# TensorE's written order: ready tasks of the loaded tile shape first, value products held back somewhat

## The chip, the cores and the metric

One Trainium2 chip; the kernel runs on one of its cores. The metric is device microseconds of one execution (us). The kernel before was timed in three runs; the median counts.

## What is computed

One encoder layer over two requests with the same weights, 4096 and 2048 tokens of 1024 features. Cut to what matters here:

```python
proj = rms_norm(x, norm_g) @ w_in                       # 1024 -> 3072 columns, split into the heads' parts
ya = neighbourhood_attention(qa, ka, va, rpb) * silu(na_g)   # 6 heads, 8 rows x 16 columns of a 64-wide grid
yb = windowed_gqa(qb, kb, vb, sink) * silu(wg)               # 6 query heads, 2 key heads, |t-s| <= 128
yc = memory_attention(qc, km, vm) * silu(mg)                 # 4 heads into 256 memory tokens
return x + concatenate([ya, yb, yc]) @ w_out
```

Every attention is a score product, a softmax over the keys and a value product. Queries and keys are normalised per head before the scores.

## The kernel before, in words

The tokens are worked off in 24 groups of 256 (16 of the first request, 8 of the second), each of two blocks of 128. Every matrix product is done in float16 pieces, a high and a low part of each operand, as three products that add up in one PSUM bank.

The first stage holds the weights for neighbourhood and memory attention. Per block it turns the input over on TensorE, four 128x128 transposes at a time (label xT, L527), projects it (labels pga and pgb of 512 columns and pgv of 384, L302 to L305: 24 matmuls each), normalises queries and keys on VectorE and GpSimd, and turns those over on TensorE (qT, L729). Per group there are then six units of neighbourhood attention: three head pairs by two pairs of column blocks. A unit is a score product on TensorE (qk, L903), bias and maximum on VectorE (L920), the exponential on ScalarE (L930), the scaling into a high and a low part on ScalarE and VectorE (L956, L965), one transposing DMA from SP's queue that writes the tile pt (L971), and the value product on TensorE (pv, L986), which waits for that DMA. Memory attention has the same chain with the labels mqk (L1042), mpT (L1092, tile ptm) and mpv (L1104), two of each per group. The raw attention results go out to HBM and are read again in the second stage, which has windowed attention (wqk, L1321; wpv, L1373), the gates (gate, L1270 to L1272), a projection of 320 columns (tok, L302 to L305 on wa and x) and the output projection (out, L1448 to L1450).

Nothing of this order is written out by hand. The class Plan keeps a list of tasks, each with an engine, a planned duration, a priority, the tasks that it needs and the buffers that it takes and gives back. Its run() goes through planned time: whenever an engine is free, it takes from that engine's ready tasks the one with the lowest priority number whose buffers are free, records its instructions, and marks the engine busy for the planned duration. A task with a slack above zero becomes ready that many planned microseconds after its last need is met. The order in which tasks are recorded is the order in which each engine works at run time; there every instruction waits only for its data. SP's DMA queue is such an engine too, and it issues in the recorded order.

TensorE's matmuls come in four shapes of array use, given in the profile as rows*columns: 128*128 for projections, gates, outputs and transposes, 64*64 for qk, 64*128 for mqk and wqk, and 128*64 for pv, mpv and wpv (96 rows in part of pv). The plan before knows nothing of them. Buffers that matter: four banks for scores (sc), two for value products (po), two for projections (pj, a third from the second stage on), four pt tiles.

Of the kernel before, what the change touches and what calls it, by code (L numbers as in the profile page):

```python
# [41 lines left out]


class Task:
    __slots__ = ("eng", "dur", "fn", "prio", "lat", "acq", "rel", "nd", "succ", "idx", "label", "slack", "xf", "start", "run", "need")

# [3 lines left out]
         "rcp": -0.1, "sc1": 2.9, "sc3": -1.24, "tab": 0.82, "ttr": -0.2, "vld": 0.2, "vst": -1.0, "w2l": -0.07,  # L52
         "wh": 3.15, "wl": 2.66, "wload": 0.43, "wmax": -1.05, "wpv": -0.5, "wqk": -1.0, "wsq": 0.93, "x": -0.53,
         "x2": -1.0,  "xrs": -0.04, "xss": 0.55, "xst": 1.74}


class Plan:
# [11 lines left out]
    def add(self, eng, dur, fn, deps=(), prio=0.0, lat=None, acq=(), rel=(), label="", slack=0.0, xf=0.0):  # L69


        t = Task()
        t.eng = t.run = eng
        t.dur, t.fn, t.prio = dur, fn, prio + SHIFT.get(label, 0.0)
        t.lat = {"pe": 0.2, "dve": 0.13, "act": 0.13, "pool": 0.16, "free": 0.01}.get(eng, 0.1) if lat is None else lat
        t.acq, t.rel, t.succ = tuple(acq), tuple(rel), []
        names = [a[0] if isinstance(a, tuple) else a for a in acq]
        t.need = tuple((a, names.count(a)) for a in dict.fromkeys(names))
        t.idx, t.label, t.xf, t.slack, t.start = len(self.tasks), label, xf, slack, None
        if label.endswith("T"):  # L80
            t.xf *= 1.5
        if eng == "sp" and xf > 0:
            t.dur = (0.63 if label.endswith("T") else 0.45) * round(dur / 0.1)
        ds = [d for d in deps if d is not None]
        t.nd = len(ds)
        for d in ds:
            d.succ.append(t)
        self.tasks.append(t)
        return t
# [21 lines left out]
    def run(self):  # L111
        avail = self.avail = dict(self.caps)
        ready = {t.eng: [] for t in self.tasks}
        busy = {}
# [17 lines left out]
        now = 0.0  # L132
        done = 0
        dma_free = 0.0
        while done < len(self.tasks):
            progress = True
            while progress:
                progress = False
                for e, q in ready.items():
                    if busy.get(e, 0.0) > now or not q:  # L140
                        continue
                    skipped = []
                    pick = None
                    while q and pick is None and len(skipped) < 25:
                        item = heapq.heappop(q)
                        if all(avail[a] >= n for a, n in item[2].need):
                            pick = item[2]
                        else:
                            skipped.append(item)
                    for s in skipped:  # L150
                        heapq.heappush(q, s)
                    if pick is None:
                        continue
                    progress = True
                    self.acquire(pick)
                    pick.start = now
                    self.emit(pick)
                    busy[e] = now + pick.dur
                    at(busy[e], FREE, pick)
                    if pick.xf > 0:  # L160

                        at(now + (0.71 if pick.label.endswith("T") else 0.53 if e == "sp" else pick.dur) + 0.65, MOVE, pick)
                        if pick.label.endswith("T"):
                            busy[e] = 1e9
                    else:
                        at(now + pick.dur + pick.lat, DONE, pick)
            if not ev:
                left = [t.label for q in ready.values() for _, _, t in q][:20]
                raise RuntimeError(f"no progress at {now}: {left} {avail}")
            now = ev[0][0]  # L170
            while ev and ev[0][0] <= now:
                _, _, kind, t = heapq.heappop(ev)
                if kind == READY:
                    heapq.heappush(ready[t.eng], (t.prio, t.idx, t))
                elif kind == MOVE:
                    dma_free = max(now, dma_free) + t.xf
                    at(dma_free + 0.95, DONE, t)
                    if t.label.endswith("T"):

                        busy[t.eng] = max(now, dma_free - 0.9)  # L180
                        at(busy[t.eng], FREE, t)
                elif kind == DONE:
                    done += 1
                    self.release(t)
                if kind == DONE or (kind == FREE and t.xf == 0):

                    for s in t.succ:
                        if (s.eng == t.eng and t.xf == 0) == (kind == FREE):
                            s.nd -= 1
                            if s.nd == 0:  # L190
                                push(now, s)
# [3 lines left out]
def build(tc, A, out, seqs):  # L195
# [64 lines left out]
    pl = Plan()  # L260
# [585 lines left out]
    for gs_ in range(NSB):  # L846
# [25 lines left out]
        for hp in range(3):  # L872
            t_pvs = []
            for ab in range(2):
# [8 lines left out]
                def f_s(us=us, cbs=cbs, kw=kw, nrows=nk // kw, kgs=kgs, hp=hp, gs_=gs_):  # L883
# [11 lines left out]
                    for r0, nr in runs:  # L895
# [7 lines left out]
                                    T.matmul(bank("sc", us[j])[64 * half:64 * half + 64, ko:ko + nr * kw], qa, ka,  # L903
                                             start=(pi == 0), stop=(pi == 2))
                        ko += nr * kw
                t_s = pl.add("pe", (3 * nk / 2.4 + 200) / 1000, f_s, base, prio=pru, acq=[("sc", u) for u in us], label="qk")
                last_qk.append(t_s)
                for h in (2 * hp, 2 * hp + 1):
                    u = (gs_, h, ab)
# [65 lines left out]
                def f_pv(gs_=gs_, hp=hp, ab=ab, kgs=kgs, edge=edge):  # L975
# [4 lines left out]
                    for half, cb in enumerate(PAIRS[ab]):  # L980
                        for ci, k in enumerate(kgs):
                            K = 96 if ab == 0 and not edge and ci == 2 else 4 * CB_KW[cb]
                            for vv in ((0, 1) if ci < nc_ - 1 else (1, 0)):
                                for j in range(2):
# [2 lines left out]
                                             st["va", k][0:K, cb, vv * 384 + h * 64:vv * 384 + h * 64 + 64],  # L987
                                             pt[0:K, j, ci, 0:2 - vv, 64 * half:64 * half + 64].rearrange("p a (r c) -> p a r c", c=16),
                                             start=(ci == 0 and vv == 0), stop=(ci == nc_ - 1 and vv == 0))
                t_pv = pl.add("pe", 0.82 * len(kgs) / 3, f_pv, [t_pT] + (vdep if ab == 0 else []) + t_pvs[-1:],  # L990
                              prio=pru, acq=[("po", gs_, hp)] if ab == 0 else [], rel=["pt"], label="pv", slack=0)
                t_pvs.append(t_pv)
                last_pv.append(t_pv)

# [27 lines left out]
    for gs_ in range(NSB):  # L1022
# [10 lines left out]
        for blk in range(2):  # L1033
            us = [(gs_, hp, blk) for hp in range(2)]

            def f_s(us=us, s=s, gs_=gs_, blk=blk):

                for j in range(2):
                    for pi, (qv, kv) in enumerate(((0, 0), (0, 1), (1, 0))):
                        for hp in range(2):  # L1040
# [1 line left out]
                            T.matmul(bank("sc", "m", us[hp])[:, 256 * j:256 * j + 256],  # L1042
                                     st["qn", 2 * gs_ + blk][prt, j, qv, :],
                                     mkv_t[s][0][prt, 2 * kv + j, :], start=(pi == 0), stop=(pi == 2))
            t_s = pl.add("pe", 0.85, f_s, [qm_done[2 * gs_ + blk], t_T1] + t_mk, prio=prm + blk / 2.0, acq=[("sc", "m", u) for u in us],
                         label="mqk")
            mqk.append(t_s)
            t_sb.append(t_s)
        for hp in range(2):
# [47 lines left out]
            def f_pv(gs_=gs_, hp=hp, s=s):  # L1097
                po = bank("po", "m", gs_, hp)[:, 0:256]
                pt = st["ptm", gs_, hp]
                for ci in range(2):  # L1100
                    for pi, (pp, vv) in enumerate(((0, 0), (0, 1), (1, 0))):
                        for j in range(2):
                            h = hp + 2 * j
                            T.matmul(po[64 * j:64 * j + 64, :], mkv_t[s][1][:, ci, vv, h * 64:h * 64 + 64],  # L1104
                                     pt[:, j * 4 + pp * 2 + ci, :], start=(ci == 0 and pi == 0), stop=(ci == 1 and pi == 2))
            t_pv = pl.add("pe", 0.82, f_pv, t_pts, prio=prm + hp / 2 + 0.25, acq=[("po", "m", gs_, hp)], rel=["ptm"], label="mpv")
            mem_use.append(t_pv)
            ym_use.append(t_pv)

# [178 lines left out]
    for nb in range(NB):  # L1288
# [10 lines left out]
        for jh in range(6):  # L1299
# [4 lines left out]
            if kv == 0:  # L1304
                us = [(nb, j), (nb, 3 + j)]

                def f_s(us=us, kbs=kbs, nb=nb, j=j):
# [9 lines left out]
                    for r0, nr in runs:  # L1317
                        for pi, (qv, kk) in enumerate(((0, 0), (0, 1), (1, 0))):
                            for v in range(2):
# [1 line left out]
                                T.matmul(bank("sc", "w", us[v])[:, o:o + nr * P], st["qT", nb][prt, 3 * qv + j, :],  # L1321
                                         st["ring2"][prt, kk, r0 * P:(r0 + nr) * P], start=(pi == 0), stop=(pi == 2))
                        o += nr * P
                t_s = pl.add("pe", (3 * nk / 2.4 + 220) / 1000, f_s, [k_done[k] for k in kbs] + [q2_done[nb], t_T3], prio=pru,
                             acq=[("sc", "w", u_) for u_ in us], label="wqk")
                win_qk[nb].append(t_s)

# [39 lines left out]
        def f_pv(nb=nb, kbs=kbs, nch=nch):  # L1367
            po = bank("po", "w", nb)
            pt = st["ptw", nb]
            for ci, k in enumerate(kbs):  # L1370
                for pi, (pp, vv) in enumerate(((0, 0), (0, 1), (1, 0))):
                    for kv in range(2):
# [1 line left out]
                                 st["vw", k][:, vv, 64 * kv:64 * kv + 64],  # L1374
                                 pt[:, pp * nch + ci, 3 * kv:3 * kv + 3, :],
                                 start=(ci == 0 and pi == 0), stop=(ci == nch - 1 and pi == 2))
        t_pv = pl.add("pe", 0.188 * 3 * nch, f_pv, t_pts + [v2_done[k] for k in kbs], prio=prw + 0.5, acq=[("po", "w", nb)], rel=["pt2"], label="wpv")
        win_pv[nb] = t_pv
        pl.add("free", 0.0, lambda: None, win_qk[nb], rel=["qT2"], label="f")

# [177 lines left out]
```

## Time and profile before

| | before |
|---|---|
| median of 3 runs | 2723.16 us (2718.52 to 2727.7) |
| the profiled execution's own time | 2732.95 us |
| its span, first to last instruction | 2731.1 us |
| mean granted TensorE clock | 0.978 |
| TensorE busy | 2590.1 us (95%) |
| VectorE, ScalarE, GpSimd busy | 1879.7, 1272.5, 543.4 us |

A row of a timeline gives start and length of an instruction or of a run of like ones, and in brackets how long the engine stood idle before it and what ended that. The lengths of matmuls overlap: how fast TensorE goes is read from the distance of the starts. PE is TensorE, DVE VectorE, ACT ScalarE, POOL GpSimd, SP the queue that issues most DMAs. The first stage runs to about 1250 us of the span, the second from there; from about 1180 us the last units of the first overlap with the first projections of the second.

### The profile page before, as it was taken

Reading aid. Unit: us, or ns where it says so; the run is one execution under the profiler, and the core shown is the slowest. Engines: PE = TensorE matmul, PEld = TensorE weight load, DVE = VectorE, ACT = ScalarE, POOL = GpSimd, SP = SyncE. Lnnn points to the kernel's source line nnn. Section 1 sums busy time; section 2 is a strip of 40 time slices with the busy share of each in tenths; the row PEclk is TensorE's granted clock in tenths of the full one; section 3 lists DMA queues with packets and bytes.
Section 4 is the critical chain, followed back from the end, with each engine's and each line's share of the span. In section 5 each row is a group of like instructions: output and inputs, shape, how many; then the busy total and the mean of one; then the engine's idle time right before and its main releaser. Section 6 shows DMA issues by size and latency. Waiting matters only on the chain.

```text
span 2731.1 us, 58589 instructions
## 1 busy us (share of the span) xinstructions
PE 2590.1 (95%) x22150; PEld 1600.3 (59%) x22150; DVE 1879.7 (69%) x5370; ACT 1272.5 (47%) x3685; POOL 543.4 (20%) x738
## 2 busy tenths in 40 slices
PE   5989888999998899978999999999999999999999
PEld 3545454555554555556666666666666666666665
DVE  6477777888777778885865665666666656566664
ACT  7456555666666667673433333333333333333332
POOL 2553233333322543321000000000000000000000
PEclk9999999999999999988999999999999999999999
DMA  5488997989998998899645444454454435455443
GB/s 182 141 160 175 190 194 186 188 191 201 206 198 181 212 212 168 169 211 261 143 101 105 100 107 106 110 122 112 111 113 104 104 90 106 106 112 122 109 95 76
DMA packets 707467, 401.38 MB, mean 147 GB/s; under 512 B 617648, under 2 KB 654160, under 8 KB 706544
## 3 DMA queue, kind: packets, MB, share of 16 engines
q1 hardware_dynamic: 691312, 347.10, 60.7%
q0 software_dynamic: 15872, 50.55, 5.4%
q8 instruction: 173, 2.83, 0.4%
q14 instruction: 110, 0.90, 0.1%
HBM read 160.54 MB, written 87.03 MB: 91 GB/s over the span
## 4 chain that ended last, share of the span: by engine, by line
PE 56%; DMA 1%; DVE 1%; issue 0%; ACT 0%; POOL 0%; SPq 0%; DVEq 0%; ACTq 0%; POOLq 0%
PE bank L1270 7%; PE bank L1448 6%; PE bank L1271 6%; PE bank L1272 6%; PE bank L1449 6%; PE bank L1450 6%; PE bank L302 4%; PE bank L303 4%; PE bank L305 4%; PE bank L1321 3%; PE bank L1373 3%; DMA pt<-phl 1%; DVE phl L965 0%; PE bank L986 0%; DVE pf L920 0%
## 5 line engine op out<-in xcount | busy, mean ns | idle before, releaser
L1270 PE MATMUL bank<-x,wb 128*128 128x256 f16 x1152 | 315.2, 274 | 0.0
L1271 PE MATMUL bank<-x,wb 128*128 128x256 f16 x1152 | 314.0, 273 | 0.0
L1272 PE MATMUL bank<-x,wa 128*128 128x256 f16 x1152 | 314.0, 273 | 0.0
L1338 ACT ACTIVATE pf<-pf,sm 128x384 f32<-128x384 f32 (+1 forms) x288 | 172.6, 599 | 300.6 <-DVE sm L1332 299.5
L302 PE MATMUL bank<-wa,xT 128*128 128x512 f16 x768 | 299.3, 390 | 4.4 <-DVE vhl L689 3.8
L303 PE MATMUL bank<-wa,xT 128*128 128x512 f16 x768 | 297.9, 388 | 0.7 <-DVE wa L364 0.6
L1448 PE MATMUL bank<-wo,yT 128*128 128x512 f16 x768 | 291.3, 379 | 0.0
L1449 PE MATMUL bank<-wo,yT 128*128 128x512 f16 x768 | 291.1, 379 | 0.0
L1450 PE MATMUL bank<-wo,yT 128*128 128x512 f16 x768 | 291.1, 379 | 0.0
L309 POOL TENSOR_TENSOR r<-r,wA 128x8 f32<-128x8 f32 x48 | 10.3, 215 | 1276.3 <-DVE r L1223 1276.3
L1277 ACT ACTIVATE tg<-bank,hg 128x256 f32<-128x256 f32 x192 | 89.6, 467 | 364.0 <-PE bank L1272 364.0
L311 POOL TENSOR_TENSOR r<-r,mhalf 128x16 f32<-128x16 f32 (+2 forms) x100 | 223.8, 2238 | 7.8
L930 ACT ACTIVATE pf<-pf,sm 128x288 f32<-128x288 f32 (+3 forms) x288 | 156.1, 543 | 128.0 <-DVE sm L920 125.9
L302 PE MATMUL bank<-wa,x 128*128 128x320 f16 x768 | 213.3, 301 | 1.0 <-DMA x<-xTd 1.0
L303 PE MATMUL bank<-wa,x 128*128 128x320 f16 x768 | 213.0, 301 | 0.0
L1463 DVE SCALAR_TENSOR_TENSOR xr<-bank,oc,xr 128x512 f32<-128x512 f32 x96 | 71.9, 749 | 197.8 <-PE bank L1450 197.8
L1332 DVE CUSTOM_DVE_ANT_0 pf<-bank,wtab,nsink 128x384 f32<-128x384 f32 (+1 forms) x288 | 163.9, 599 | 58.6 <-PE bank L1321 58.5
L302 PEld LDWEIGHTS <-xT 128*128 128x128 f16 x1152 | 115.2, 100 | 124.8 <-issue 25.1
L303 PEld LDWEIGHTS <-xT 128*128 128x128 f16 x1152 | 115.1, 100 | 114.5 <-issue 16.3
L305 PE MATMUL bank<-wa,xT 128*128 128x512 f16 x768 | 181.4, 379 | 0.0
L305 PEld LDWEIGHTS <-xT 128*128 128x128 f16 x1152 | 112.8, 98 | 115.7 <-issue 0.3
L1355 DVE SCALAR_TENSOR_TENSOR phl<-pf,sm,phl 128x384 f16<-128x384 f32 (+1 forms) x288 | 174.3, 605 | 8.5
(261 smaller groups left out, 5746.1 us busy)
## 6 DMA issues: line engine op xcount, KB each, us to landing
xTd<-xT POOLq DMA_DIRECT2D x48, 512.0 KB, 4.7
x<-xTd SPq DMA_DIRECT2D x48, 512.0 KB
out<-xr SPq DMA_DIRECT2D x48, 512.0 KB
xx<-in_x_prompt SPq DMA_DIRECT2D x32, 512.0 KB
xr<-in_x_prompt SPq DMA_DIRECT2D x32, 512.0 KB
od<-oev POOLq DMA_DIRECT2D x120, 128.0 KB, 3.8
ot<-od SPq DMA_DIRECT2D x120, 128.0 KB
vd<-vhl POOLq DMA_DIRECT2D x48, 192.0 KB, 4.4
```

The source lines that it names most:

```text
L302: T.matmul(ps, xt[:, kk], wh[:, kk, cols], start=(kk == 0), stop=False)
L303: T.matmul(ps, xt[:, kk], wl[:, kk, cols], start=False, stop=False)
L305: T.matmul(ps, xt[:, NK + kk], wh[:, kk, cols], start=False, stop=(kk == NK - 1))
L311: G.tensor_tensor(out=r, in0=r, in1=mhalf[:, 0:n], op=ALU.pow)
L1270: T.matmul(pv, wh, x[:, :, kk, :], start=(kk == 0), stop=False)
L1271: T.matmul(pv, wh, x[:, :, NK + kk, :], start=False, stop=False)
L1272: T.matmul(pv, wl, x[:, :, kk, :], start=False, stop=(kk == NK - 1))
L1338: S.activation(out=pf[:, 0:nk], in_=pf[:, 0:nk], func=AF.Exp, scale=-1.0, bias=sm[:, 0:1], accum_out=sm[:, 1:2])
L1355: V.scalar_tensor_tensor(out=phl[:, nk:2 * nk], in0=st["pfw", u][:, 0:nk], scalar=st["smw", u][:, 3:4], in1=phl[:, 0:nk], op0=ALU.mult, op ...
L1448: T.matmul(ps, yT[:, 0, ts_], st["wo0"][:, c, cs], start=(ci == 0), stop=False)
L1449: T.matmul(ps, yT[:, 0, ts_], st["wo1"][:, c, cs], start=False, stop=False)
L1450: T.matmul(ps, yT[:, 1, ts_], st["wo0"][:, c, cs], start=False, stop=(ci == 7))
```

## The change

Three things, all inside the plan; no instruction is added, removed or resized.

First, a task on TensorE has a shape. When the pick of lowest priority has another shape than the task before it, run() looks on through the ready tasks up to 0.3 above that priority and takes the first of the loaded shape instead, if there is one whose buffers are free. A pick of another shape is planned 0.095 us longer.

Second, the planned durations of qk, pv, mqk, mpv, wqk and wpv are smaller.

Third, pv and mpv get a slack of 2.0: they enter TensorE's ready list 2 planned microseconds after their transposing DMA is planned to have landed.

```diff
+SHAPES = {"qk": "64x64", "mqk": "64x128", "wqk": "64x128", "pv": "128x64", "mpv": "128x64", "wpv": "128x64"}
+DRY = 0.095
+
+KEEP = 0.3
...
+        shape = "128x128"
         while done < len(self.tasks):
...
+                    if pick is not None and e == "pe" and pick.shape != shape:
+
+                        first = pick
+                        while q and pick is first and q[0][0] <= first.prio + KEEP:
+                            item = heapq.heappop(q)
+                            if item[2].shape == shape and all(avail[a] >= n for a, n in item[2].need):
+                                pick = item[2]
+                                skipped.append((first.prio, first.idx, first))
+                            else:
+                                skipped.append(item)
...
+                    dry = 0.0
+                    if e == "pe":
+                        dry = DRY if pick.shape != shape else 0.0
+                        shape = pick.shape
...
-                    busy[e] = now + pick.dur
+                    busy[e] = now + pick.dur + dry
...
-                t_s = pl.add("pe", (3 * nk / 2.4 + 200) / 1000, f_s, base, prio=pru, acq=[("sc", u) for u in us], label="qk")
+                t_s = pl.add("pe", (3 * nk / 2.4 + 20) / 1000, f_s, base, prio=pru, acq=[("sc", u) for u in us], label="qk")
...
-                t_pv = pl.add("pe", 0.82 * len(kgs) / 3, f_pv, [t_pT] + (vdep if ab == 0 else []) + t_pvs[-1:],
-                              prio=pru, acq=[("po", gs_, hp)] if ab == 0 else [], rel=["pt"], label="pv", slack=0)
+                t_pv = pl.add("pe", 0.5 * len(kgs) / 3, f_pv, [t_pT] + (vdep if ab == 0 else []) + t_pvs[-1:],
+                              prio=pru, acq=[("po", gs_, hp)] if ab == 0 else [], rel=["pt"], label="pv", slack=2.0)
...
-            t_pv = pl.add("pe", 0.82, f_pv, t_pts, prio=prm + hp / 2 + 0.25, acq=[("po", "m", gs_, hp)], rel=["ptm"], label="mpv")
+            t_pv = pl.add("pe", 0.66, f_pv, t_pts, prio=prm + hp / 2 + 0.25, acq=[("po", "m", gs_, hp)], rel=["ptm"], label="mpv",
+                          slack=2.0)
```

The changed file is 24 lines longer, so its line numbers differ from those of before: L903 is L926, L986 is L1009, L1104 is L1127, L302 is L325, L1270 is L1294, L1373 is L1397.

What this does to TensorE's row is seen at two places. The first is in group 7 of the first stage (groups counted from 0), from the score product of its fifth unit to the value product of that unit, the 47th of the 144 pv. Before, TensorE's row has there, with the first row of each task and "..." for its others (L903 is qk, L1104 mpv, L302 pgv on wb and pga on wa, L986 pv, L729 qT, L527 xT):

```order
L903 MATMUL bank5_68<-ring_628,qT_5297 64x256
...
L1104 MATMUL bank7_70<-ptm_6769,mkv_629 64x256
...
L302 MATMUL bank1_64<-wb_350,xT_6826 128x384
...
L986 MATMUL bank6_69<-pt_7234,va_4759 64x8x16
...
L903 MATMUL bank5_68<-ring_628,qT_5297 64x192
...
L903 MATMUL bank3_66<-ring_628,qT_6067 64x128
...
L302 MATMUL bank0_63<-wa_349,xT_7160 128x512
...
L729 MATMUL bank5_68<-ident_275,raw_6835 128x2x4x16 x3
...
L986 MATMUL bank7_70<-pt_7520,va_4759 64x8x16
...
L527 MATMUL bank2_65<-ident_275,xx_359 128x128 x4
```

The same stretch in the changed kernel's TensorE row, from the same score product to the same value product (L926 is qk, L1127 mpv, L325 pga, pgb and pgv, L550 xT, L1065 mqk, L1009 pv, L752 qT; left out beside the tasks' other rows are a second mpv ahead of the one shown, the second xT and qT, and the second of two neighbouring qk):

```order
L926 MATMUL bank5_68<-ring_628,qT_5259 64x256
...
L1127 MATMUL bank7_70<-ptm_6719,mkv_629 64x256
...
L325 MATMUL bank0_63<-wa_349,xT_6903 128x512
...
L550 MATMUL bank4_67<-ident_275,xx_359 128x128 x4
...
L1065 MATMUL bank2_65<-mkv_629,qn_6609 128x256
...
L325 MATMUL bank1_64<-wa_349,xT_6903 128x512
...
L1009 MATMUL bank6_69<-pt_7242,va_4870 64x8x16
...
L926 MATMUL bank4_67<-ring_628,qT_5259 64x192
...
L325 MATMUL bank0_63<-wb_350,xT_6903 128x384
...
L752 MATMUL bank4_67<-ident_275,raw_6898 128x2x4x16 x3
...
L1009 MATMUL bank6_69<-pt_7279,va_4870 64x8x16
...
L1009 MATMUL bank7_70<-pt_7331,va_4870 64x8x16
```

Before, one long projection of 512 columns and one of 384 stand between the unit's score and value product; now two of 512 and one of 384 do, and the value product follows directly on that of the unit before it, in the same shape.

The second place is in the second stage, around the value product of window block 23. TensorE's row before, first row of each task (L1270 is gate, L1321 wqk, L302 tok, L1373 wpv):

```order
L1270 MATMUL bank3_66<-x2_26066,wb2_16755 128x256
...
L1321 MATMUL bank4_67<-ring2_16901,qT2_26481 128x128
...
L1270 MATMUL bank1_64<-x2_26066,wb2_16755 128x256
...
L302 MATMUL bank0_63<-wa2_16617,x2_26814 128x320
...
L302 MATMUL bank3_66<-wa2_16617,x2_26814 128x320
...
L1373 MATMUL bank6_69<-pt2_26573,vw_25638 64x384
...
L1270 MATMUL bank1_64<-x2_26066,wb2_16755 128x256
```

The same place in the changed kernel (L1294 is gate, L325 tok, L1345 wqk, L1397 wpv):

```order
L1294 MATMUL bank0_63<-x2_26007,wb2_16744 128x256
...
L325 MATMUL bank1_64<-wa2_16614,x2_26749 128x320
...
L325 MATMUL bank2_65<-wa2_16614,x2_26749 128x320
...
L1294 MATMUL bank0_63<-x2_26007,wb2_16744 128x256
...
L1294 MATMUL bank1_64<-x2_26007,wb2_16744 128x256
...
L1345 MATMUL bank3_66<-ring2_16918,qT2_26453 128x128
...
L1397 MATMUL bank7_70<-pt2_26723,vw_25616 64x384
...
L1294 MATMUL bank2_65<-x2_26007,wb2_16744 128x256
```

Before, the score product and the value product each stand alone between tasks of the full shape, four changes of shape; now they stand together, three changes. Counted over TensorE's whole row, matmul by matmul, the shape changes 849 times before (451 in the first stage, 38 in its overlap with the second, 359 in the rest, one at a seam between them) and 752 times now (408, 28, 315 and one).

More of the change, by code (lines that the diff above doesn't have):

```diff
@@ L44 @@
 class Task:
-    __slots__ = ("eng", "dur", "fn", "prio", "lat", "acq", "rel", "nd", "succ", "idx", "label", "slack", "xf", "start", "run", "need")
+    __slots__ = ("eng", "dur", "fn", "prio", "lat", "acq", "rel", "nd", "succ", "idx", "label", "slack", "xf", "start", "run", "need", "shape")
 SHIFT = {"bE": 0.02, "c": 1.22, "eva": 0.26, "evb": -0.01, "exp": -0.1, "g2": 1.94, "hi": 0.3, "kg": -1.0,
@@ L77, in add @@
         names = [a[0] if isinstance(a, tuple) else a for a in acq]
+        t.shape = SHAPES.get(label, "128x128") if eng == "pe" else ""
         t.need = tuple((a, names.count(a)) for a in dict.fromkeys(names))
@@ L165, in run @@
                     else:
-                        at(now + pick.dur + pick.lat, DONE, pick)
+                        at(now + pick.dur + dry + pick.lat, DONE, pick)
             if not ev:
@@ L1044, in f_s @@
                                      mkv_t[s][0][prt, 2 * kv + j, :], start=(pi == 0), stop=(pi == 2))
-            t_s = pl.add("pe", 0.85, f_s, [qm_done[2 * gs_ + blk], t_T1] + t_mk, prio=prm + blk / 2.0, acq=[("sc", "m", u) for u in us],
+            t_s = pl.add("pe", 0.66, f_s, [qm_done[2 * gs_ + blk], t_T1] + t_mk, prio=prm + blk / 2.0, acq=[("sc", "m", u) for u in us],
                          label="mqk")
@@ L1323, in f_s @@
                         o += nr * P
-                t_s = pl.add("pe", (3 * nk / 2.4 + 220) / 1000, f_s, [k_done[k] for k in kbs] + [q2_done[nb], t_T3], prio=pru,
+                t_s = pl.add("pe", (3 * nk / 2.4 + 20) / 1000, f_s, [k_done[k] for k in kbs] + [q2_done[nb], t_T3], prio=pru,
                              acq=[("sc", "w", u_) for u_ in us], label="wqk")
@@ L1376, in f_pv @@
                                  start=(ci == 0 and pi == 0), stop=(ci == nch - 1 and pi == 2))
-        t_pv = pl.add("pe", 0.188 * 3 * nch, f_pv, t_pts + [v2_done[k] for k in kbs], prio=prw + 0.5, acq=[("po", "w", nb)], rel=["pt2"], label="wpv")
+        t_pv = pl.add("pe", 0.162 * 3 * nch, f_pv, t_pts + [v2_done[k] for k in kbs], prio=prw + 0.5, acq=[("po", "w", nb)], rel=["pt2"], label="wpv")
         win_pv[nb] = t_pv
```

## The prediction

> **What bounds the kernel now.** I read the page first, then the busy time by stretch.
>
> ```profile
> span 2731.1 us, 58589 instructions
> PE   5989888999998899978999999999999999999999
> DMA  5488997989998998899645444454454435455443
> 130.00:1180.00 1050.00, 965.91 (x9968) 558.09 (x9967) 826.54 (x2255) 659.75 (x1834) 385.13 (x505) 0.97 0.90 190
> 1180.00:1260.00 80.00, 56.03 (x776) 37.67 (x774) 54.05 (x188) 46.04 (x148) 17.64 (x30) 0.72 1.08 218
> 1260.00:2731.00 1471.00, 1466.49 (x10900) 950.99 (x10897) 924.99 (x2746) 491.94 (x1565) 94.29 (x136) 1.00 0.49 111
> ```
>
> The columns behind the length are the busy times of PE, weight load, DVE, ACT and POOL, the granted clock, the share of the DMA engines and GB/s. TensorE is the bound in all three stretches, in different ways. From 1260 us on it is busy 1466.49 of 1471 us at clock 1.00 with the DMA engines at 0.49: there only less TensorE work helps. From 130 to 1180 us it is busy 965.91 of 1050 us, so 84 us are waits, and the clock is 0.97, which is at most 0.03 x 1050 = 31 us of lost speed. DVE is at 826.54 / 1050 = 79%, the DMA engines at 0.90. The seam from 1180 to 1260 us is bad in every way: 24 us idle, clock 0.72, DMA at 1.08. What ends TensorE's waits in the first of these stretches, in total, times and longest:
>
> ```profile
> PE bank L986 <- DMA pt<-phl: 37.6, 26, 6.6
> PE bank L1104 <- DMA ptm<-phm: 20.4, 9, 4.6
> PE bank L903 <- DVE sm L920: 5.4, 2, 4.1
> PE bank L527 <- DVE sm L920: 4.3, 3, 2.1
> PE bank L729 <- DVE raw L707: 4.2, 2, 2.8
> ```
>
> 37.6 + 20.4 = 58.0 us in 35 waits are value products that stand in TensorE's row before their transposed tile has landed; everything queued behind them on TensorE, projections that have their data included, stands still too. The other 26 us are scattered over small causes. In the seam the same wait takes 19.2 us:
>
> ```profile
> PE bank L986 <- DMA pt<-phl: 19.0, 13, 3.8
> PE bank L1104 <- DMA ptm<-phm: 0.2, 1, 0.2
> ```
>
> **The change, part by part.** One piece of TensorE's timeline prices the first two parts.
>
> ```profile
> 555.82 0.65 PE L903 MATMUL bank<-ring,qT 64*64 64x256 f16 x24
> 556.40 0.85 PE L1104 MATMUL bank<-ptm,mkv 128*64 128x256 f16 x12
> 557.18 0.34 PE L302 MATMUL bank<-wb,xT 128*128 128x384 f16 x1
> ...
> 559.63 0.33 PE L303 MATMUL bank<-wb,xT 128*128 128x384 f16 x1
> 559.79 1.46 PE L305 MATMUL bank<-wb,xT 128*128 128x384 f16 x8
> 561.18 0.72 PE L986 MATMUL bank<-pt,va 96*64 96x128 f16 x24
> 561.83 1.02 PE L903 MATMUL bank<-ring,qT 64*64 64x192 f16 x48
> 562.79 0.39 PE L302 MATMUL bank<-wa,xT 128*128 128x512 f16 x1
> ...
> 566.04 0.38 PE L303 MATMUL bank<-wa,xT 128*128 128x512 f16 x1
> 566.25 1.89 PE L305 MATMUL bank<-wa,xT 128*128 128x512 f16 x8
> 567.98 1.04 PE L729 MATMUL bank<-ident,raw 128*128 128x128 f32 x8
> 570.68 0.72 PE L986 MATMUL bank<-pt,va 128*64 128x128 f16 x24 [1.67 <-DMA pt<-phl]
> 571.33 0.87 PE L527 MATMUL bank<-ident,xx 128*128 128x128 f32 x6
> ```
>
> *Fewer changes of shape.* Sixteen matmuls of 512 columns start between 562.79 and 566.25, so 0.216 us each; the eight of L305 should take 8 x 0.216 = 1.73 us, and the transposes behind them, of the same 128*128, start exactly 1.73 us later (566.25 to 567.98). Sixteen of 384 columns take 557.18 to 559.79, 0.163 each; eight should take 1.31 us, but the value product behind them, of 128*64, starts after 1.39. A change of shape therefore costs some 0.09 us. The second stage says the same with shorter matmuls:
>
> ```profile
> 2020.32 0.27 PE L1271 MATMUL bank<-x,wgc 128*128 128x256 f16 x1
> 2020.42 0.27 PE L1272 MATMUL bank<-x,wgc 128*128 128x256 f16 x1
> 2020.63 0.66 PE L1321 MATMUL bank<-ring,qT 64*128 64x384 f16 x6
> ```
>
> 0.10 from gate to gate, 0.21 from gate to score product: 0.10 to 0.11 us. With 0.095 and 849 - 752 = 97 fewer changes the saving is 9.2 us. Of it 359 - 315 = 44 changes, 4.2 us, fall in the second stage, where TensorE never waits and nothing can hide or take them back; the other 5 us fall where TensorE waits at times. The Trainium skill (TensorE: Matmul & The Clock Gate, part 2, the drain step) has the last column of a matmul take about 128 array cycles to leave; if a change of shape waited for just that, my estimate from its figure is 53 ns, and the term would be 5 us. The rows above show nearly twice that, so they are used.
>
> *Value products later.* The order puts more work of TensorE between a unit's scores and its value product. For the unit whose wait is shown (570.68), the row before has, from 556.40 to the wait's begin at 570.68 - 1.67 = 569.01, mpv 0.78, pgv 4.00, pv 0.65, two qk 0.96, pga 5.19, two qT 1.03: 12.6 us. In the changed order the same unit has two mpv 1.56, pga 5.19, two xT (taken as two qT) 1.03, mqk (taken as one mpv) 0.78, pgb 5.19, pv 0.65, two qk 0.96, pgv 4.00, two qT 1.03, pv 0.65: 21.0 us, 8.4 more, against a wait of 1.67. I did the same sum for all 144 units of neighbourhood attention: the middle value goes from 13.7 to 19.2 us. For memory attention it goes from 19.6 to 21.2 us only. A wait goes where the order adds at least as much work as the wait is long. Of the 58.0 us this leaves seven places: the longest pv wait of 6.6 us, whose distance shrinks by 5 us, some 1.8 us at three other pv, and 9.2 us at three mpv (two without added work, one with 1.7 us for a wait of 4.6). So 17.6 us stay and 40.4 go.
>
> *The clock.* Long waits cost twice. Five of those that go are over 3 us and are followed by half clock:
>
> ```profile
> core 0: us, PE busy (x), PEclk, DMA share, GB/s
> 194.50:201.30 6.80, 5.99 (x51) 0.50 0.72 156
> 283.20:286.60 3.40, 3.40 (x12) 0.50 0.65 160
> 464.10:470.90 6.80, 6.29 (x41) 0.50 0.68 195
> 778.10:781.60 3.50, 3.28 (x19) 0.51 0.74 167
> 982.90:986.40 3.50, 3.50 (x29) 0.51 0.72 162
> 730.40:733.80 3.40, 3.31 (x19) 0.51 0.71 159
> ```
>
> The first five are 24 us at half speed, so 12 us at most; less the parts in which TensorE stood still I take 10. The sixth follows a wait that I leave in place:
>
> ```profile
> 730.50 1.49 PE L1104 MATMUL bank<-ptm,mkv 128*64 128x256 f16 x12 [2.47 <-DMA ptm<-phm]
> ```
>
> The Trainium skill (TensorE: Matmul & The Clock Gate, part 1) says that the clock falls only after at least one idle window of about 3.4 us. By that rule only the longest waits would bring clock back and this term would shrink to some 6 us, a total 4 us higher. The row at 730.50 speaks against it: 2.47 us were enough here.
>
> *What comes back.* A TensorE that no longer waits for tiles runs up against its other sources sooner: score products that wait for a bank, transposes for normalised rows. Those waits are 26 us today with DVE at 79%. Taking 40 + 10 + 5 = 55 us from a stretch of 1050 raises DVE to 826.54 / 995 = 83% and the DMA engines to about 0.95. The return lies between nothing and the whole 55. DVE keeps 17% idle, and the seam shows that the DMA engines can stand at 1.08, so I take a value near the low end, 14 us, half again on the 26 us there are.
>
> *Kept at nothing.* The smaller planned durations only move the order. In the second stage the order changes too, but what covers it is wide: in TensorE's work, summed in the same way, a window value product starts 28 us after its last score product before and 29 in the changed order (in the tenth with the least 27 and 24), and 49 and 38 us after its first; no wait stands there now. If that cover went, 48 value products at 1 us would be the price. The seam keeps its 19 us: its distances grow by only 1 to 7 us where chains take far longer than TensorE has work; I give it 10 us either way.
>
> The sum against the profiled execution, which took 2732.95 us (span 2731.1 and 1.85 around it): -9.2 - 40.4 - 10 + 14 = -45.6, or 2687.4 us. The runs' median is 2723.16, 9.8 us lower than that execution; the same saving from the median gives **2677.6 us**, -1.7%.
>
> **The rivals.**
>
> *Something else paces the first stage, chance 0.18.* If DVE's chain or the transfers set its pace, the value product's wait only moves to the next instruction that needs them: qk for its bank, xT and qT for their rows. For it: DMA at 0.90, and all the small waits on DVE. Against it: TensorE has the smallest idle share of all engines there, and DVE is idle for 223 of 1050 us. Then only the 9.2 us of shapes remain, 2714 us. The Trainium skill (TensorEngine Tiling (Array Packing), Performance Considerations, PSUM Bottleneck) warns of this: tiling makes TensorE faster but not the emptying of PSUM, which may then be the limit. The waits of L903 for L920 above, 5.4 us, are that limit's present size.
>
> *Slower: pt tiles run out, chance 0.08.* A value product that comes later keeps its pt tile longer, and there are four. The fifth transposing DMA then waits at the head of SP's queue for TensorE, with every load and store behind it. Today that is nearly nothing beside SP's waits for DVE:
>
> ```profile
> SPq L971 <- DVE phl L965: 108.3, 44, 6.8
> SPq L971 <- PE bank L986: 2.8, 3, 1.4
> ```
>
> A unit comes every 1050 / 144 = 7.3 us, so 5.5 us more of holding is 0.75 of a tile on average; it decides where a tile is held for over 4 x 7.3 = 29 us. If a third of the 144 DMAs then waited as long as a value product does today (58.0 / 35 = 1.7 us) and handed it on, that is +80 us; less the 45.6, the kernel takes 2757 us.
>
> *All waits for tiles and all half-clock stretches go, nothing comes back, chance 0.08.* 9.2 + 58.0 + 31 = 98 us: 2625 us. For it: every distance but some twenty grows. Against it: the seven places above.
>
> *The change does nothing to the order, chance 0:* both parts are seen in it.
>
> **How the numbers follow.** My forecast has 0.66; by itself it reaches from 2650 (nothing comes back, the seam gains 10, a little more of the clock) to 2708 (two thirds of the tile waits and clock come back). The range of 2645 to 2715 leaves out the slower case, most of the full gain and half of the paced case. About 0.3%, 8 us, is what a measurement of this kernel can tell from no change, so faster means below 2715. Faster: 0.66 + 0.08 + nearly half of 0.18 = 0.82. Same: the rest of the paced case, 0.10. Slower: 0.08.
>
> **What would show it.** In the changed profile: TensorE's waits for pt and ptm between 130 us and the seam at some 18 us in place of 58; the clock there at 0.98 or more; value products in neighbouring pairs with no 0.09 us between them; in the second stage no wait on TensorE and a stretch some 4 us shorter; the seam some 40 us earlier. The forecast is wrong if waits of qk, xT or qT for DVE grow by 40 us (first rival), if SP's queue waits for L1009 by tens of us (second), or if the first stage ends where it did.

## The result, and the profile after

The changed kernel is slower: 2747.97 us median of five runs (2743.16 to 2753.68) against 2726.86 for the kernel before, now a median of five runs too, a ratio of 1.0078 with a 95% interval of 1.0064 to 1.0093. I had forecast 1.7% faster. The profiled execution has a span of 2751.8 us against 2731.1, 20.7 us more.

The page of the changed kernel, and its busy time by stretch with the same columns as before:

```profile
span 2751.8 us, 58515 instructions
PE   6998899998898989987999999999999999999999
DMA  5497989988998988899745444445544434445542
```

```profile
130.00:1180.00 1050.00, 953.96 (x9710) 550.45 (x9710) 806.11 (x2197) 644.79 (x1792) 377.45 (x496) 0.95 0.90 185
```

In the same 1050 us TensorE did 9710 matmuls in place of 9968, stood idle for 96 us in place of 84, and had a clock of 0.95 in place of 0.97. A good mark for the border of the stages is the first gate matmul. The rows of the gate's first line, before (L1270) and after (L1294), with shortest, middle and longest length in ns and the first and last start:

```profile
L1270 PE MATMUL bank<-x,wb x1152: 272/273/284, 1263.5 to 2690.9; 128*128 128x256 f16 x192
L1294 PE MATMUL bank<-x,wb x1152: 272/273/283, 1287.7 to 2709.5; 128*128 128x256 f16 x192
```

The first gate starts 24.2 us later, and from there to the end it takes 2751.8 - 1287.7 = 1464.1 us against 2731.1 - 1263.5 = 1467.6. So the second stage gained 3.5 us, and the first lost 24.2, although its matmuls are the same and change shape some 50 times less. What ends TensorE's waits now, the five largest from 130 to 1190 us (the two lines of tiles are the same up to 1180):

```profile
PE bank L1009 <- DMA pt<-phl: 36.1, 14, 7.3
PE bank L1127 <- DMA ptm<-phm: 18.6, 6, 6.5
PE bank L550 <- DVE xx L540: 7.9, 3, 4.5
PE bank L752 <- ACT pfm L1087: 4.8, 2, 4.5
PE bank L926 <- ACT pfm L1087: 4.6, 7, 1.5
```

The waits for tiles went from 35 to 20 in number and stayed the same in sum, 54.7 us against 58.0: many short ones are gone and the ones left are longer, 2.7 us on average in place of 1.7. The unit that served as my example has indeed lost its wait: its value product is the second half of the run of 48 here, without a bracket, and nothing is lost between the two units of one shape. But between its scores, which end at 532.0, and that product TensorE now stands still elsewhere, at a value product of memory attention that waits for VectorE (the first row).

```profile
537.05 1.49 PE L1127 MATMUL bank<-ptm,mkv 128*64 128x256 f16 x12 [2.84 <-DVE oev L1025]
...
558.30 1.04 PE L752 MATMUL bank<-ident,raw 128*128 128x128 f32 x8
559.26 1.25 PE L1009 MATMUL bank<-pt,va 96*64 96x128 f16 x48
```

The longest wait stands at a unit that did not wait before, the 97th pv, though 26 us of TensorE's work lie between its scores and its value product in place of 20. The value product, SP's queue just ahead of it, and the busy times around it (columns as above):

```profile
984.53 0.85 PE L1009 MATMUL bank<-pt,va 128*64 128x128 f16 x16 [7.32 <-DMA pt<-phl]
```

```profile
965.26 2.77 SPq L792 DMA_DIRECT2D va<-vd  x4
968.14 1.06 SPq L854 DMA_DIRECT2D w2do<-xhl  x2
969.30 7.45 SPq L994 DMA_TRANSPOSE pt<-phl  x1
976.80 1.22 SPq L523 DMA_DIRECT2D xx<-in_x_sample  x1
```

```profile
965.00:975.00 10.00, 10.00 (x75) 5.09 (x68) 9.11 (x23) 5.26 (x18) 5.13 (x8) 1.00 1.32 183
975.00:985.00 10.00, 2.68 (x24) 1.35 (x23) 1.85 (x7) 1.89 (x4) 0.00 (x0) 0.73 0.75 182
```

Six loads and stores went out just ahead of the transposing DMA; the DMA share is 1.32 (it adds up the time of all packets, so it can pass 1), the issue of the one transposing DMA holds SP's queue for 7.45 us (the middle one takes 2.1), and its data land only around 984.5, some 15 us after the issue began. In the ten microseconds before that every engine is nearly still, GpSimd altogether, and the clock falls. This is not a value product that stands too early in TensorE's row; the transfer itself was late.

### The profile page after: what moved, and what is told of

It is laid out like the page before. It is cut to its first block, busy times and chain, and to the rows that moved or that the text cites. A ratio compares the mean times of both kernels' runs of the same rounds, so it can differ in the third digit from the quotient of the medians.

```text
span 2751.8 us, 58515 instructions
## 1 busy us (share of the span) xinstructions
PE 2594.9 (94%) x22150; PEld 1610.3 (59%) x22150; DVE 1879.5 (68%) x5370; ACT 1270.1 (46%) x3685; POOL 543.7 (20%) x738
## 4 chain that ended last, share of the span: by engine, by line
PE 55%; DMA 2%; DVE 1%; ACT 0%; issue 0%; SPq 0%; POOL 0%; DVEq 0%; ACTq 0%
PE bank L1294 6%; PE bank L1472 6%; PE bank L1295 6%; PE bank L1296 6%; PE bank L1474 6%; PE bank L1473 6%; PE bank L325 4%; PE bank L326 4%; PE bank L328 4%; PE bank L1345 3%; PE bank L1397 3%; DMA pt<-phl 2%; PE bank L926 0%; PE bank L1009 0%; DMA x<-xTd 0%
## 5 line engine op out<-in xcount | busy, mean ns | idle before, releaser
L1294 PE MATMUL bank<-x,wb 128*128 128x256 f16 x1152 | 315.0, 273 | 0.0
L325 PE MATMUL bank<-wa,xT 128*128 128x512 f16 x768 | 299.8, 390 | 4.7 <-DVE vhl L712 3.8
L953 ACT ACTIVATE pf<-pf,sm 128x352 f32<-128x352 f32 (+3 forms) x288 | 156.9, 546 | 127.8 <-DVE sm L943 125.5
L325 PE MATMUL bank<-wa,x 128*128 128x320 f16 x768 | 213.9, 302 | 1.1 <-DMA x<-xTd 1.1
L325 PEld LDWEIGHTS <-xT 128*128 128x128 f16 x1152 | 115.9, 101 | 130.4 <-issue 30.3
```

Of the source, the lines that this page charges most:

```text
L325: T.matmul(ps, xt[:, kk], wh[:, kk, cols], start=(kk == 0), stop=False)
L1294: T.matmul(pv, wh, x[:, :, kk, :], start=(kk == 0), stop=False)
```

## The experiments

Two theories went into the first runs. *One part loses*: one of the three parts (smaller planned durations, pick by shape, slack) does the harm. *Any redrawn order loses*: every change of any planning number draws another order of the first stage, and the order of before is simply a better one than most. A "redraw" below is a kernel in which one planned duration is moved by 0.01 us and nothing else. First gate and span are those of the profiled executions, which stand up to 8 us off the median of their kernel.

| kernel | median us | ratio to before, 95% interval | first gate | span |
|---|---|---|---|---|
| kernel before | 2726.86 | 1 | 1263.5 | 2731.1 |
| changed kernel | 2747.97 | 1.0078 (1.0064 to 1.0093) | 1287.7 | 2751.8 |
| b_pick: pick by shape alone | 2774.63 | 1.0184 (1.0165 to 1.0203) | 1304.5 | 2772.1 |
| b_durations: durations alone | 2744.68 | 1.0074 (1.0048 to 1.0099) | 1276.6 | 2744.7 |
| b_slack: slack alone | 2748.65 | 1.0096 (1.0074 to 1.0118) | 1286.2 | 2754.0 |
| a_no_slack: changed, no slack | 2772.57 | 1.0160 (1.0124 to 1.0196) | 1314.2 | 2778.0 |
| a_no_pick: changed, no pick | 2754.86 | 1.0096 (1.0070 to 1.0121) | 1278.3 | 2745.8 |
| a_old_durations: changed, old durations | 2723.39 | 0.9988 (0.9973 to 1.0004) | 1255.3 | 2720.1 |
| b_nudge1, redraw of before | 2749.71 | 1.0095 (1.0077 to 1.0114) | 1272.4 | 2748.2 |
| b_nudge2, redraw of before | 2766.46 | 1.0137 (1.0111 to 1.0162) | 1291.5 | 2767.6 |
| b_nudge5, redraw of before | 2754.78 | 1.0088 (1.0067 to 1.0109) | 1286.0 | 2754.1 |
| a_nudge1, redraw of the changed kernel | 2749.97 | 1.0082 (1.0056 to 1.0109) | 1285.7 | 2749.5 |
| a_nudge2, redraw of the changed kernel | 2733.95 | 1.0029 (1.0012 to 1.0045) | 1268.4 | 2732.4 |
| a_nudge5, redraw of the changed kernel | 2759.27 | 1.0120 (1.0097 to 1.0142) | 1293.8 | 2757.6 |

**The parts alone.** In the kernel before, one part of the change is put in and the other two left out. For b_pick, for example, the cut against the changed kernel is ("..." stands for lines left out, here and below):

```diff
-DRY = 0.095
+DRY = 0.0
...
-(3 * nk / 2.4 + 20) / 1000        # and the five other planned durations
+(3 * nk / 2.4 + 200) / 1000       # as before
...
-label="pv", slack=2.0)
+label="pv", slack=0)
```

Expected of b_pick: 

> The kernel before with the pick by shape alone: planned durations and slack as before, no planned cost of a change of shape. TensorE's row changes shape 776 times in place of 849, worth 73 x 0.095 = 7 us. Theory 'one part loses' (the smaller planned durations are the part): no loss here, 2715 to 2728 us. Rival 'any redrawn order loses' (before's table of priorities fits its own order of the first stage, and every change of a planning number draws another): 2735 to 2755 us, with the loss in front of the first gate.

Expected of b_durations: 

> The kernel before with the smaller planned durations and the planned 0.095 us per change of shape alone, no pick by shape, no slack; 849 changes as before. 'One part loses': the whole loss, 2745 to 2760 us. 'Any redrawn order loses': 2735 to 2755 us; this run alone does not tell the two apart.

Expected of b_slack: 

> The kernel before with the slack of 2.0 of both value products alone; 850 changes of shape. 'One part loses' (the durations): the waits for tiles shrink as I had forecast and nothing else happens, 2690 to 2727 us. 'Any redrawn order loses': 2735 to 2755 us.

All three lose, by 18 to 48 us, and the one that I had thought harmless loses most, beyond the range of either theory. No single part is to blame.

**The parts taken out.** From the changed kernel one part is removed:

```diff
-KEEP = 0.3
+KEEP = -1.0       # a_no_pick; a_no_slack has slack 0, a_old_durations the old durations and DRY = 0.0
```

Expected of a_no_slack: 

> The changed kernel without the slack of the value products. 'One part loses' with the slack as the part: back to 2715 to 2727 us; with the durations as the part: as the changed kernel, 2740 to 2755. 'Any redrawn order loses': somewhere in 2720 to 2760, with no tie to the part that was taken out.

Expected of a_no_pick: 

> The changed kernel without the pick by shape: 835 changes of shape in place of 752, so 8 us more from them alone. 'One part loses' (durations): 2750 to 2762 us. 'Any redrawn order loses': 2725 to 2770, with the second stage some 4 us longer than the changed kernel's whatever the first does.

Expected of a_old_durations: 

> The changed kernel with the planned durations of before and no planned cost of a change of shape; the pick and the slack stay. 799 changes of shape. 'One part loses' (durations): the loss is gone, 2700 to 2725 us. 'Any redrawn order loses': 2725 to 2760 us.

With the old durations back the loss is gone (0.9988), as "one part loses" had it; a_no_slack, at 2772.57, is again slower than either theory had. But the same durations alone cost 18 us while slack alone costs 22 and the pick alone 48, and slack and pick together, which is what a_old_durations is, cost nothing. Parts that each lose and together don't are no parts of a sum. By the second theory a_old_durations is a redraw that came out well; the only one of these six that did.

**Redraws without the change.**

```diff
-            t = pl.add("pe", 0.45, f_T, [t, t_id], ...
+            t = pl.add("pe", 0.46, f_T, [t, t_id], ...      # nudge1; nudge2 and nudge5 move VectorE's 1.14 to 1.15 and 0.66 to 0.67
```

Expected of b_nudge1: 

> The kernel before with one planning number moved by next to nothing: the input transposes are planned at 0.46 us in place of 0.45. None of the change's three parts is in it, but 532 tasks of TensorE's row stand at another place. 'One part loses': 2718 to 2736 us, as before. 'Any redrawn order loses': 2735 to 2755 us, the waits for tiles no smaller than before's 77 us.

Expected of b_nudge2: 

> A second redraw of the kernel before without any part of the change: the reduction of the squares is planned at 1.15 us on DVE in place of 1.14; 563 tasks of TensorE's row move. 'One part loses': 2718 to 2736 us. 'Any redrawn order loses': 2735 to 2755 us.

Expected of b_nudge5: 

> A third redraw of the kernel before with no part of the change: the low part of the transposed input is planned at 0.67 us on VectorE in place of 0.66; 527 tasks of TensorE's row move. 'Any redrawn first stage loses': 2740 to 2770 us, as the two other redraws (2750 and 2766).

Three of three lose, by 0.9 to 1.4%, with nothing of the change in them; b_nudge2 by more than either theory had. Their first gates start 9 to 28 us later than before's. So the changed kernel's loss needs no cause in the change: of the 13 other orders in the table 12 are slower than before, by 0.3 to 1.8%.

**Redraws of the changed kernel.** The same three nudges on the changed kernel.

Expected of a_nudge1: 

> The changed kernel with the input transposes planned at 0.46 us in place of 0.45: 467 tasks of TensorE's row stand at another place, 760 changes of shape. 'One part loses': as the changed kernel, 2743 to 2754 us. 'Any redrawn order loses': a time of its own, off the changed kernel's by up to 20 us either way, the second stage alike within 2 us.

Expected of a_nudge2: 

> A second redraw of the changed kernel by the same nudge of 0.01 us on DVE's planned reduction: 455 tasks of TensorE's row move, 763 changes of shape. 'One part loses': 2743 to 2756 us. 'Any redrawn order loses': a time of its own within 20 us of the changed kernel's, its second stage alike.

Expected of a_nudge5: 

> A third redraw of the changed kernel, the low part of the transposed input planned at 0.67 us on VectorE in place of 0.66; 422 tasks of TensorE's row move. If the change itself is worth something beside its redraw, redraws of it stand below redraws of before (2750 and 2766) by some 10 us: 2730 to 2755 us. If it is worth nothing beside the 9 us of shapes, the two sets overlap.

With the changed kernel itself that is 2748, 2750, 2734 and 2759, a mean of 2748; redraws of before are 2750, 2766 and 2755, a mean of 2757. The two sets overlap. The mean first gate is 1283 in the redraws of before and 1284 in the four with the change: in the first stage I can see nothing that the change is worth, though with a scatter of 19 to 25 us within each set some few us would not be seen. From the first gate to the end the four take 1463.8 to 1464.1 us, steady, and the redraws of before 1468.1 to 1476.1. That part is real: before itself takes 1467.6. The other kernels of the table bear it out. Without the pick a_no_pick, b_durations and b_slack take 1467.5 to 1468.1 us; with it a_no_slack and a_old_durations take 1463.8 and 1464.8. Three rows stand apart for reasons of their own: b_nudge1 and b_nudge2 (1475.8 and 1476.1) wait 4.2 us for a gate's weights just behind the first gate and run their first 9 to 10 us from there at a clock of 0.50, and b_pick (1467.6) has 18 matmuls more behind its first gate than the others.

**No wait for tiles at all.** The orders stay as they are, but the value products of the first stage read one small tile that is filled once. The transposing DMAs are still issued, nobody reads them, and the right value products are left out of the result.

```diff
+        G.memset(one("YN", "ptz", [P, 2, P], F16), 0.5)
...
-                    pt = st["pt", gs_, hp, ab].rearrange("p (j a c) t -> p j c a t", j=2, a=2)
+                    pt = st["ptz"]
...
-                pt = st["ptm", gs_, hp]
+                pt = st["ptz"].rearrange("p a t -> p (a t)")
```

Expected of b_static: 

> The kernel before, same order on every engine, but the value products of neighbourhood and memory attention read one tile that is filled once and never written again; the transposing DMAs are still issued, and no one reads what they write. So this leaves the right value products out of the result. No value product can wait for its tile, and no transposing DMA for TensorE. Theory 'the waits for tiles set the first stage': 77 us of waits and most of 61 us of half clock's loss go, 2640 to 2670 us. Rival 'something else paces it' (the other producers' chains): the waits move to qk, xT and qT, 2700 to 2725 us.

Expected of a_static: 

> The changed kernel with the same cut: value products of the first stage read one tile that is never rewritten, so the right value products are left out. 'The waits for tiles set the first stage': 66 us of waits and part of the clock's loss go, 2650 to 2680 us. 'Something else paces it': 2725 to 2745 us, with the waits for DVE at qk, qT, xT grown by what the tiles give up.

b_static takes 2720.38 us, 0.9979 (0.9960 to 0.9998) of before; a_static 2736.71, 1.0033 (1.0017 to 1.0049) of before, 11 us under the changed kernel. Waits of 77 and 66 us are gone and bring 6 (at most 11 by the interval) and 11. TensorE's waits of b_static from 130 to 1180 us:

```profile
PE bank L527 <- DVE sm L921: 18.0, 11, 7.5
PE bank L904 <- DVE sm L921: 9.9, 7, 4.7
PE bank L904 <- ACT pfm L1065: 7.6, 10, 3.2
PE bank L1105 <- DVE oev L1003: 6.7, 3, 3.4
```

They have moved to transposes and score products (L527, L904), which wait for VectorE and ScalarE. The value product's wait was where TensorE met the pace of the stage, not what set the pace.

**What paces the first stage.** On top of b_static, once VectorE's low part of the neighbourhood units' probabilities is left out (288 instructions become tiny ones), once half of every neighbourhood unit's transposing DMA; the result lacks these parts too. Order and count of instructions stay.

```diff
-                        V.scalar_tensor_tensor(out=dl, in0=src, scalar=r, in1=dh, op0=ALU.mult, op1=ALU.subtract)
+                        V.tensor_single_scalar(st["sm", u[0], h // 2, ab][:, 4 + h % 2:5 + h % 2], r, 1.0, op=ALU.mult)
```

```diff
-                    SY.dma_start_transpose(out=tile_of("YN", ("pt", gs_, hp, ab), "pt", [P, 12, P], F16),
-                                           in_=st["phl2", gs_, hp, ab].rearrange("p j a b k -> p (j a b k)"))
+                    SY.dma_start_transpose(out=tile_of("YN", ("pt", gs_, hp, ab), "pt", [P, 12, P], F16)[:, 0:6],
+                                           in_=st["phl2", gs_, hp, ab][:, 0].rearrange("p a b k -> p (a b k)"))
```

Expected of b_static_nolo: 

> The kernel before with the static tile for the value products (right value products left out), and on top of it VectorE's low part of the neighbourhood units' probabilities left out: 288 instructions of 0.55 us become ones of about 0.1 on one column, some 130 us less work for VectorE, same order. 'VectorE's work paces the first stage': at least 60 us below the static tile's 2720, under 2660. 'The transfers pace it': 2705 to 2720, VectorE only idles more.

Expected of b_static_halfT: 

> The kernel before with the static tile for the value products (right value products left out), and each of the 144 transposing DMAs of neighbourhood attention moves one head of its two, half the packets, same order. 'The transfers pace the first stage': its DMA share falls by a tenth and the time by 40 us or more, under 2680. 'VectorE's work paces it': 2710 to 2720.

b_static_nolo takes 2711.5 us, b_static_halfT 2681.37 (two runs each; 0.9935 and 0.9825 of before, with intervals of 0.9910 to 0.9960 and 0.9799 to 0.9850). The stretch from 130 to 1180 us in b_static, b_static_nolo and b_static_halfT, in that order, and the first gates of the three:

```profile
130.00:1180.00 1050.00, 979.24 (x10125) 563.99 (x10125) 835.06 (x2286) 665.82 (x1863) 386.67 (x508) 0.97 0.91 192
```

```profile
130.00:1180.00 1050.00, 984.21 (x10182) 566.33 (x10182) 750.16 (x2300) 669.58 (x1875) 386.92 (x509) 0.97 0.92 193
```

```profile
130.00:1180.00 1050.00, 994.45 (x10551) 578.48 (x10551) 868.54 (x2405) 692.91 (x1948) 397.88 (x520) 0.97 0.79 174
```

```profile
L1271 PE MATMUL bank<-x,wb x1152: 272/273/285, 1247.0 to 2674.2; 128*128 128x256 f16 x192
```

```profile
L1271 PE MATMUL bank<-x,wb x1152: 272/273/284, 1241.8 to 2669.1; 128*128 128x256 f16 x192
```

```profile
L1271 PE MATMUL bank<-x,wb x1152: 272/273/284, 1209.5 to 2636.8; 128*128 128x256 f16 x192
```

Taking 85 us from VectorE's 835 moves the first gate by 5 us and the time by 9. Halving the neighbourhood units' transposes, which takes the DMA share from 0.91 to 0.79, moves it by 37.5 us and the time by 39, and TensorE, VectorE, ScalarE and GpSimd all get through more work in the same stretch. So transfers pace the first stage, as shown with the static tile in before's order; with the real tiles it was not tried. Whether by what the DMA engines can move or by how long a transfer sits in the queue, these runs do not part.

**Only the second stage redrawn.** The kernel before with the pick switched on from planned time 1165 us, after the last task of the first stage:

```diff
-                    if pick is not None and e == "pe" and pick.shape != shape:
+                    if pick is not None and e == "pe" and now > 1165.0 and pick.shape != shape:
```

Expected of c_second_only: 

> The kernel before with the pick by shape from planned time 1165 us on alone, no other part of the change: every engine's order of the first stage stays as it was up to the first gate, the second stage is drawn anew with 806 changes of shape in all in place of 849. 'The redrawn first stage is what loses': 43 x 0.095 = 4 us faster than before, 2719 to 2725 us, no wait of TensorE in the second stage. 'Any redraw loses, the second stage's too': 2727 us or more.

2725.44 us, 0.9991 (0.9977 to 1.0005), which alone tells neither from the other. The profile does: the first gate starts at 1267.2 in this execution, 3.7 us later in an unchanged order, and the rest takes 2731.9 - 1267.2 = 1464.7 us against 1467.6. The pick is worth 2.9 us there, and executions of one kernel differ by more.

**A plan that knows slower transfers.** If transfers pace the stage, the number that a redraw lacks is their length. The changed kernel with every transfer planned 15% longer:

```diff
-        t.idx, t.label, t.xf, t.slack, t.start = len(self.tasks), label, xf, slack, None
+        t.idx, t.label, t.xf, t.slack, t.start = len(self.tasks), label, 1.15 * xf, slack, None
```

Expected of a_dma: 

> The changed kernel with every transfer planned 15% longer, nothing else. Theory 'the plan lets transfers land too early': the order leaves more work ahead of each consumer, TensorE's waits for DMA fall below 30 us and the time to 2700 to 2725 us. 'A redraw is a draw': 2730 to 2765 us like the others.

2700.09 us, 0.9899 (0.9880 to 0.9919) of before: 1.0% faster than the kernel before and 1.7% faster than the changed one, 34 us below the best redraw of the changed kernel. TensorE's waits from 130 to 1180 us, the four largest, the first gate, and the busy times of that stretch:

```profile
PE bank L1127 <- DMA ptm<-phm: 12.2, 6, 3.4
PE bank L752 <- DVE qn L320: 8.3, 2, 7.1
PE bank L1065 <- DVE xT L563: 7.5, 2, 7.2
PE bank L1009 <- DMA pt<-phl: 7.1, 5, 2.5
```

```profile
L1294 PE MATMUL bank<-x,wb x1152: 272/273/283, 1234.5 to 2657.7; 128*128 128x256 f16 x192
```

```profile
130.00:1180.00 1050.00, 979.61 (x10274) 568.81 (x10274) 855.41 (x2341) 680.73 (x1904) 389.14 (x516) 0.96 0.93 194
```

The waits for tiles are 19.3 us in place of 54.7, which is what I had forecast for the change (18), and the first gate comes 53 us earlier than in the changed kernel, with more done by every compute engine in the 1050 us than there and a DMA share of 0.93. It is one draw; that its distance from the others is due to the 15% and not to luck is likely by the scatter of the redraws (2734 to 2759) and not shown by a second draw.

## Why the prediction was wrong, point by point

*The shapes* were right in the second stage: 4.2 us forecast, 3.5 measured by the first gate and the end, 0.08 us for each of the 44 changes; no wait on TensorE worth naming there (0.8 us in all). In the first stage the 5 us can't be seen beside the rest.

*Value products later* is the step that failed, in the sentence "A wait goes where the order adds at least as much work as the wait is long". I took the landing of a tile as fixed and moved only the value product. But the new order moved the transposing DMAs, and the loads and stores between which they queue, as well: the distance grew by 5.5 us in the middle and the landing moved too. Followed through both traces unit by unit, the middle pt tile lands 17.0 us after its scores ended in place of 13.9: its DMA is issued later (10.7 us after the scores in place of 8.6 in the middle), and more tiles land late behind the issue (over 8 us for 18 of the 144 in place of 6). Of the 41 pv of the whole first stage that waited before, 32 no longer wait; 15 others now do. 40.4 us were to go; 3.3 went (58.0 to 54.7). I had laid TensorE's row beside TensorE's row, and had not laid SP's.

*The clock* was to give 10 us back. It fell from 0.97 to 0.95 in the same stretch, a further 0.02 x 1050 = 21 us at most, while the waits for tiles became fewer and longer. These waits are not all that sets it: a_dma has 19.3 us of them and a clock of 0.96.

*What comes back* would have failed next: it was set to 14 of 55 us by VectorE's 79%. With all waits for tiles taken away only 6 of 77 us were kept, so nearly all of them come back, and not through the amount of VectorE's work. The first rival had the mechanism, "something else paces the first stage"; I gave it 0.18 because no engine was busier than TensorE. A DMA share of 0.90 stood in the quoted rows; I read 1.08 at the seam as room above it. The row from 965 to 975 us at 1.32, with SP's queue held, shows what such a number can mean for one transfer.

*The forecast's missing case* is the slower side. The second rival, SP's queue waiting for pt tiles, is not it:

```profile
SPq L994 <- PE bank L1009: 9.0, 9, 2.9
```

That is 9.0 us against 2.8, not tens. What made the kernel slower than 2714 us is, by the redraws, that before's order of the first stage is an unusually good one, and the change gave it up: 0 of 3 redraws of before keep its time. Why it is so good, whether its table of priorities was fitted to it by measuring, is not shown by these runs.

## What to carry to other kernels

Where a plan sets the order, a change of one planning number is two changes: what it means to do, and a new draw of everything else. Measure what a draw is worth first, with nudges that mean nothing (here 23 to 42 us of 2727), and judge the change by the mean of several draws or in a stage that the draw leaves alone. And before counting a wait as a gain, take the wait away by itself, with data that are always ready: here 77 us of waits were worth 6.

## What was not expected of the hardware

One transposing DMA behind six other transfers held SP's queue for 7.45 us where the middle one takes 2.1, and all compute engines ran nearly dry behind it within ten microseconds; the longest hold in the kernel before is 8.2 us. And transfers paced a stage whose mean DMA share was no more than 0.91 over a millisecond: with half of the neighbourhood units' transposes, at 0.79 and in the same order, the stage ended 37.5 us earlier.
